# Order of the products in the first mixture of experts: latents and context in groups of four row blocks

## The chip, the cores and the metric

The kernel runs on one core of one Trainium2 chip. The metric is the device time of one launch in microseconds (us). Before the change three runs took 2783.61, 2788.53 and 2795.34 us; the median is 2788.53 us. The engines are named as in the profile: PE is TensorE (matmuls), PEld its weight loads, DVE is VectorE, ACT is ScalarE, POOL is GpSimd, SP is SyncE, which here only issues DMAs.

## The reference, cut to what matters

The model is a two-layer hybrid backbone on 512 latent tokens and 256 context tokens of width 1024, all in float32. Layer 0 mixes tokens with neighbourhood attention, layer 1 with a bidirectional recurrence; after each comes a mixture of experts with 16 experts. Each expert chooses the tokens it likes best: 64 latents (2 * 512 / 16), and in layer 0 also 32 context tokens (2 * 256 / 16) with the same weights. Layer 1 has no mixture for the context. What one expert computes:

```
xin = h[idx]                                   # 64 latents, or 32 context tokens, of width 1024
hid = silu(xin @ w1) * (xin @ w3)              # w1, w3: 1024 x 1024
y   = (hid @ w2) * gate                        # w2: 1024 x 1024; then added back at the rows idx
```

The weights of one expert are three 1024 x 1024 float32 matrices, 12 MiB; all 16 experts are read in full in each layer.

## The kernel before

The program runs in four stages: neighbourhood attention, the first mixture (layer 0, latents and context), the recurrence, the second mixture (layer 1, latents only). The change touches `expert` alone (lines 744 to 811), which both mixtures call. In the second one `xinc` is None, so there are no context products.

**Weights.** `load_weights` brings one tile `wm` of 1 MiB: two row blocks of 128 rows (two values of k) of one matrix. An expert has twelve of them: numbers 0 to 7 are w1 and w3 by turns, 8 to 11 are w2. Its caller issues the load of tile i + 10 from SP right behind the matmuls that read tile i, because in the first mixture the tiles lie in a ring of ten buffers. A load can start only when the last reader of the tile ten places before it is done. SP takes its loads in order.

**The first two products.** For every k of 0 to 7 the latents' part of `expert` makes four matmuls (line 759): w1 into P1 and w3 into P3, each in two halves of 512 columns. The stationary operand is 64 columns wide (64 latents), so the two halves stand side by side in two column tiles of the array and write PSUM partitions 0 to 63 and 64 to 127. The context's part (line 763) makes four matmuls into Pc with 32 stationary columns each, in four column tiles side by side. The stationary operands are slices of `xin` and `xinc`, gathered and transposed tokens. In the profile every float32 matmul shows as two records, so one k is 8 records of line 759 and 8 of line 763.

**Between them.** ACT takes the SiLU of P1 (line 768), DVE multiplies by P3 (line 769), PE transposes the result (line 71, `tp` from `hid`), ACT copies it to `hidT` (line 774). For the context the same with `hidc` (lines 777, 778) and `hidTc` (line 783).

**The third product.** For every k two matmuls for the latents (line 792, 4 records) and four of 256 columns for the context (line 796, 8 records).

**Around it.** Every second expert `gather` fetches the next 128 latents, every fourth the next 128 context tokens. `scatter` (line 829, 128 stationary columns) adds the results back into the rows.

**Who sets the order.** The code gives each engine a program order, but the instructions of this stage are laid out by a planner at build time: it goes through a modelled time line and gives an engine the earliest instruction, in program order, whose inputs the model holds ready. So matmuls of a later line are found ahead of an earlier one that was not ready in the model. The order is fixed before the run; the chip executes it as it stands. The recurrence has its order for PE, DVE and ACT written by hand.

Of the kernel before, what the change touches and what calls it, by code (L numbers as in the profile page):

```python
# [33 lines left out]
KD = 8  # L34
# [34 lines left out]
def transpose(S, out, in_):  # L69
    n = in_.shape[0]  # L70
    S.nc.tensor.transpose(out, in_, S.ident[:n, :n])  # L71
# [550 lines left out]
def load_weights(S, R, i, q=None):  # L622

    e, j = divmod(i, 12)
    if e >= E:
        return
    n, kk = (("moe_w1", "moe_w3")[j % 2], j // 2) if j < 8 else ("moe_w2", j - 8)
    a = R.ring[i % len(R.ring)]
    w = R.wm[a].tile([P, 2, D], F32, name="wm")
    (q or S.nc.sync).dma_start(w, S.I[n][R.l, e, kk * 256:(kk + 1) * 256].rearrange("(k p) n -> p k n", p=P))  # L630
    R.w[i] = w
# [112 lines left out]
def expert(S, R, e, xin, xinc, wk, psh, Y, YC):  # L744
    nc = S.nc
    ctxs = xinc is not None
    P1 = psh.tile([P, 512], F32, name="P1")
    P3 = psh.tile([P, 512], F32, name="P3")
    Pc = psh.tile([P, 512], F32, name="Pc") if ctxs else None
    cl = slice(64 * (e % 2), 64 * (e % 2) + 64)  # L750
    cc = slice(32 * (e % 4), 32 * (e % 4) + 32)
    for kk in range(4):
        ws = [R.w.pop(12 * e + 2 * kk + i) for i in range(2)]
        for k2 in range(2):
            k = 2 * kk + k2
            st, sp = k == 0, k == KD - 1
            for w, ps in zip(ws, (P1, P3)):
                for hf in range(2):
                    nc.tensor.matmul(ps[64 * hf:64 * hf + 64], xin[:, k, cl], w[:, k2, hf * 512:(hf + 1) * 512],  # L759
                                     start=st, stop=sp)  # L760
            if ctxs:
                for i in range(4):
                    nc.tensor.matmul(Pc[32 * i:32 * i + 32], xinc[:, k, cc],  # L763
                                     ws[i // 2][:, k2, (i % 2) * 512:(i % 2 + 1) * 512], start=st, stop=sp)
        for i in range(2):
            load_weights(S, R, 12 * e + 2 * kk + i + len(R.ring))
    hid = wk.tile([P, 512], F32, name="hid")
    nc.scalar.activation(hid, P1, AF.Silu)  # L768
    nc.vector.tensor_tensor(hid, P3, hid, op=ALU.mult)  # L769
    pt = S.ps_tp.tile([P, 512], F32, name="tp")  # L770
    for c in range(4):
        transpose(S, pt[:, c * P:(c + 1) * P], hid[:, c * P:(c + 1) * P])
    hT = wk.tile([P, 4, 2, CAPL], F32, name="hidT")
    nc.scalar.activation(hT.rearrange("p c h s -> p (c h s)"), pt, AF.Copy)  # L774
    if ctxs:
        hc = wk.tile([P, 512], F32, name="hidc")
        nc.scalar.activation(hc[64:128], Pc[0:64], AF.Silu)
        nc.vector.tensor_tensor(hc[0:64], Pc[64:128], hc[64:128], op=ALU.mult)
        pt = S.ps_tp.tile([P, 512], F32, name="tp")
        for c in range(4):  # L780
            transpose(S, pt[:, c * 64:(c + 1) * 64], hc[0:64, c * P:(c + 1) * P])
        hTc = wk.tile([P, 4, 2, CAPC], F32, name="hidTc")
        nc.scalar.activation(hTc.rearrange("p c h s -> p (c h s)"), pt[:, :256], AF.Copy)
    py = S.ps_mm.tile([P, 512], F32, name="mm")
    pyc = S.ps_mm.tile([P, 512], F32, name="mm") if ctxs else None
    for kk in range(4):
        w = R.w.pop(12 * e + 8 + kk)
        for k2 in range(2):
            k = 2 * kk + k2
            st, sp = k == 0, k == KD - 1  # L790
            for hf in range(2):
                nc.tensor.matmul(py[64 * hf:64 * hf + 64], hT[:, k % 4, k // 4, :], w[:, k2, hf * 512:(hf + 1) * 512],  # L792
                                 start=st, stop=sp)
            if ctxs:
                for i in range(4):
                    nc.tensor.matmul(pyc[32 * i:32 * i + 32, :256], hTc[:, k % 4, k // 4, :],
                                     w[:, k2, i * 256:(i + 1) * 256], start=st, stop=sp)
        load_weights(S, R, 12 * e + 8 + kk + len(R.ring))
    o = 64 * (e % 2)
    for hf in range(2):  # L800
        r = slice(64 * hf, 64 * hf + 64)
        c = slice(512 * hf, 512 * hf + 512)
        nc.vector.scalar_tensor_tensor(Y[o:o + 64, c], py[r], R.g[0][r, e:e + 1], S.gt2[0][r, c],  # L803
                                       op0=ALU.mult, op1=ALU.mult)
    if ctxs:
        o = 32 * (e % 4)
        for i in range(4):
            r = slice(32 * i, 32 * i + 32)
            c = slice(256 * i, 256 * i + 256)
            nc.vector.scalar_tensor_tensor(YC[o:o + 32, c], pyc[r, :256], R.g[1][r, e:e + 1], S.gt2[1][r, c],  # L810
                                           op0=ALU.mult, op1=ALU.mult)
# [21 lines left out]
def phase_moe(S, R):  # L833
    tc, l = S.tc, R.l
    ctxs = l == 0
    with ExitStack() as es:
        n0, n1 = WRING[l]
        R.wm.append(es.enter_context(tc.tile_pool(name="wmq", bufs=n1, reuse_waits="tile")))
        wk = es.enter_context(tc.tile_pool(name="moew", bufs=2, reuse_waits="tile"))
        R.ring += [len(R.wm) - 1] * n1  # L840
        m = max(n0, EARLY[l])
        for i in range(n0, m):
            load_weights(S, R, i)
        with tc.issue_after(R.last.ins):
            for i in range(m, n0 + n1):
                load_weights(S, R, i, S.nc.gpsimd)
        psh = es.enter_context(tc.tile_pool(name="psh", bufs=1, space=PSUM))
        xc = None
        for e in range(E):
            if e % 2 == 0:  # L850
                xl = gather(S, R, e // 2, 0)
                Y = wk.tile([P, D], F32, name="Y")
            if e % 4 == 0 and ctxs:
                xc = gather(S, R, e // 4, 1)
                YC = wk.tile([P, D], F32, name="YC", bufs=1)
            expert(S, R, e, xl, xc, wk, psh, Y, YC if ctxs else None)
            if e % 2 == 1:
                scatter(S, R, wk, R.ids[0][:, e // 2:e // 2 + 1], Y, S.X[:NLT])
            if e % 4 == 3 and ctxs:
                scatter(S, R, wk, R.ids[1][:, e // 4:e // 4 + 1], YC, S.X[NLT:])  # L860
    R.es.close()
# [1050 lines left out]
```

## Time and profile before

| what | value |
|---|---|
| median of three runs | 2788.53 us (2783.61 to 2795.34) |
| the profiled execution's own time | 2783.66 us |
| its span in the profile | 2781.7 us |
| PE busy, share of the span | 2475.8 us, 89% |
| DVE, ACT, POOL busy | 48%, 36%, 21% |
| granted TensorE clock, mean | 0.955 of full speed |
| bytes moved by DMA | 637.62 MB, 229 GB/s over the span |
| first mixture, first to last product | 631.5 us to 1284.5 us |
| second mixture, end of the last products of line 759 | 2757.2 us |

The span is the first to the last instruction of one profiled execution; its own time is 2 us longer and includes what lies around the span. A busy time is the time in which an engine had at least one instruction under way. For PE that says little about speed, since matmuls overlap and their ends are modelled, so below the distance from the start of one group of matmuls to the start of the next is read.

### The profile page before, as it was taken

The numbers are of one execution on the slowest core, as the hardware profiler recorded it, in microseconds if no ns is written. First come the engines' busy times: TensorE is split into PE (matmuls) and PEld (weight loads), VectorE is DVE, ScalarE is ACT, GpSimd is POOL, SyncE is SP. The second block draws the span as 40 slices with busy tenths as digits, with TensorE's granted clock in tenths as the row PEclk, the third lists the DMA queues.
The fourth block names the chain that finished last, engine by engine and source line by source line (L and its number), as shares of the span: only waits on it lengthen the run. The fifth ranks groups of instructions, "written<-read, shape, count | busy, mean of one in ns | idle before, by whom it ended". The sixth has DMA issues, their size and how long they took to land. (4 is left out here: it accounts for less than half of the span.)

```text
span 2781.7 us, 43985 instructions
## 1 busy us (share of the span) xinstructions
PE 2475.8 (89%) x16803; PEld 1534.7 (55%) x16803; DVE 1337.5 (48%) x2987; ACT 1004.4 (36%) x2121; POOL 595.9 (21%) x855
## 2 busy tenths in 40 slices
PE   6999999889999999997689697999999959988887
PEld 4876778782333322333389596777778843322222
DVE  6656665551222211215978745676676762211221
ACT  3555566531110100113266535676665421000000
POOL 1110000121000000001556535665555200000000
PEclk9999999989999999998899898999999959999999
DMA  8655530329788879774157966556654279999998
GB/s 244 146 157 183 159 114 17 113 103 372 271 345 319 325 287 364 277 292 166 69 176 247 270 158 136 130 127 145 129 115 127 61 274 373 409 409 409 409 409 334
DMA packets 427521, 637.62 MB, mean 229 GB/s; under 512 B 133824, under 2 KB 301056, under 8 KB 427312
## 3 DMA queue, kind: packets, MB, share of 16 engines
q1 hardware_dynamic: 419328, 609.11, 64.7%
q0 software_dynamic: 7984, 25.70, 2.5%
q8 instruction: 134, 2.20, 0.3%
q14 instruction: 75, 0.61, 0.1%
HBM read 565.11 MB, written 53.88 MB: 223 GB/s over the span
## 5 line engine op out<-in xcount | busy, mean ns | idle before, releaser
L759 PE MATMUL P<-wm,xin 128*64 128x512 f32 x2048 | 503.3, 607 | 42.1 <-DMA wm<-in_moe_w_dram 41.9
L759 PEld LDWEIGHTS P<-wm,xin 128*64 128x64 f32 x2048 | 132.8, 137 | 369.8 <-issue 270.8
L792 PE MATMUL mm<-wm,hidT 128*64 128x512 f32 x1024 | 250.8, 601 | 20.4 <-ACT hidT L774 16.1
L768 ACT ACTIVATE hid<-P 128x512 f32<-128x512 f32 x32 | 19.1, 598 | 690.1 <-PE P L759 690.1
L803 DVE SCALAR_TENSOR_TENSOR Y<-mm,gates,gt 64x512 f32<-64x512 f32 x64 | 48.0, 750 | 320.8 <-PE mm L792 320.1
L769 DVE TENSOR_TENSOR hid<-P,hid 128x512 f32<-128x512 f32 x32 | 22.1, 692 | 371.3 <-PE P L759 371.3
L731 POOL DMA_INDIRECT xg<-xnd,ii x20 | 19.1, 956 | 808.1 <-PE tp L71 521.9
L248 PE MATMUL mm<-wh,hTh 128*128 128x256 f32 x576 | 171.6, 298 | 2.5 <-ACT hTh L542 2.5
L250 PE MATMUL mm<-wh,hTl 128*128 128x256 f32 x576 | 166.7, 290 | 1.7 <-DVE hTl L545 1.7
L249 PE MATMUL mm<-wl,hTh 128*128 128x256 f32 x576 | 166.7, 290 | 0.0
L792 PEld LDWEIGHTS mm<-wm,hidT 128*64 128x64 f32 x1024 | 69.0, 136 | 159.5 <-issue 116.4
L763 PE MATMUL Pc<-wm,xin 128*32 128x512 f32 x1024 | 147.3, 602 | 0.0
L1443 POOL TENSOR_TENSOR Wi<-Wi,Ti 112x30 f32<-112x30 f32 (+14 forms) x240 | 142.1, 592 | 18.7
L1441 POOL TENSOR_TENSOR Ti<-Wi 112x30 f32<-112x30 f32 (+14 forms) x240 | 135.8, 566 | 18.2
L248 PEld LDWEIGHTS mm<-wh,hTh 128*128 128x128 f32 x576 | 112.5, 195 | 12.7 <-issue 9.1
L250 PEld LDWEIGHTS mm<-wh,hTl 128*128 128x128 f32 x576 | 112.0, 195 | 4.2 <-DVE hTl L545 2.7
L1520 PE MATMUL mm<-FR,QF 128*128 128x128 f32 (+1 forms) x768 | 113.5, 291 | 0.4 <-ACT QF L1508 0.4
L249 PEld LDWEIGHTS mm<-wl,hTh 128*128 128x128 f32 x576 | 112.6, 196 | 1.4 <-issue 1.4
L830 DVE TENSOR_TENSOR X<-mm,X 128x512 f32<-128x512 f32 x80 | 51.9, 687 | 106.1 <-PE mm L829 105.8
L1520 PEld LDWEIGHTS mm<-FR,QF 128*128 128x128 f32 x768 | 97.1, 197 | 7.4 <-ACT QF L1508 0.9
L1508 ACT ACTIVATE QF<-mm 64x256 f32<-64x256 f32 x192 | 72.9, 379 | 66.8 <-PE mm L1504 63.1
L1523 DVE TENSOR_TENSOR FT<-mm,eye 64x128 f32<-64x128 f32 x192 | 55.9, 292 | 77.4 <-ACT FT L1522 75.4
(429 smaller groups left out, 5697.3 us busy)
## 6 DMA issues: line engine op xcount, KB each, us to landing
wm<-in_moe_w_dram SPq DMA_DIRECT2D x378, 1024.0 KB
adaw<-in_ada_w_dram SPq DMA_DIRECT2D x96, 512.0 KB
wraw<-in_na_w_qkv_dram SPq DMA_DIRECT2D x32, 256.0 KB
wm<-in_moe_w_dram POOLq DMA_DIRECT2D x6, 1024.0 KB, 11.0
pkd<-sig SPq DMA_DIRECT2D x24, 256.0 KB
pkd<-kka SPq DMA_DIRECT2D x24, 256.0 KB
pkd<-av SPq DMA_DIRECT2D x24, 256.0 KB
sig<-pkd SPq DMA_DIRECT2D x16, 384.0 KB
```

Source lines behind the costliest of these rows:

```text
L248: S.nc.tensor.matmul(ps, xh, wh, start=(k == 0), stop=False)
L249: S.nc.tensor.matmul(ps, xh, wl, start=False, stop=False)
L250: S.nc.tensor.matmul(ps, xl, wh, start=False, stop=(k == n - 1))
L759: nc.tensor.matmul(ps[64 * hf:64 * hf + 64], xin[:, k, cl], w[:, k2, hf * 512:(hf + 1) * 512], start=st, stop=sp)
L763: nc.tensor.matmul(Pc[32 * i:32 * i + 32], xinc[:, k, cc], ws[i // 2][:, k2, (i % 2) * 512:(i % 2 + 1) * 512], start=st, stop=sp)
L792: nc.tensor.matmul(py[64 * hf:64 * hf + 64], hT[:, k % 4, k // 4, :], w[:, k2, hf * 512:(hf + 1) * 512], start=st, stop=sp)
L830: nc.vector.tensor_tensor(X[t][:, sl], ps, X[t][:, sl], op=ALU.add)
L1441: nc.gpsimd.tensor_tensor(t, W3[:, i + 1:32, i:i + 1].to_broadcast([112, n, i]), W3[:, i:i + 1, 0:i].to_broadcast([112, n, i]), op=ALU.mult)
L1443: nc.gpsimd.tensor_tensor(W3[:, i + 1:32, 0:i], W3[:, i + 1:32, 0:i], t, op=ALU.add)
L1508: nc.scalar.activation(QF[m][0:64, u], pq[64 * u:64 * u + 64], AF.Copy)
L1520: nc.tensor.matmul(pf[:, h, s0:], QF[m][:, u, h, :], rhs, start=True, stop=True)
L1523: nc.vector.tensor_tensor(F[64:128, :, 64:128], pf[64:128, :, 64:128], S.eye2[64:128, None, :].to_broadcast([64, 2, 64]), op=ALU.add)
```

## The change

`expert` gets a step: 4 where the context is computed, 2 where it is not. In a step the latents' matmuls of all its k come first, then the context's matmuls of the same k, then the loads that reuse the buffers of the step. Before, the turn changed at every k, and loads were issued after every second k, two tiles in the first two products (lines 765 and 766) and one for w2 (line 798). With a step of 4 four tiles are given back at once in the first two products, and two in the third. The number of matmuls, their shapes and operands stay. Without the context the loops come out in the order that they had.

```diff
-    for kk in range(4):
-        ws = [R.w.pop(12 * e + 2 * kk + i) for i in range(2)]
-        for k2 in range(2):
-            k = 2 * kk + k2
-            st, sp = k == 0, k == KD - 1
-            for w, ps in zip(ws, (P1, P3)):
+    step = 4 if ctxs else 2
+    for k0 in range(0, KD, step):
+        ws = {k: [R.w[12 * e + 2 * (k // 2) + i][:, k % 2] for i in range(2)] for k in range(k0, k0 + step)}
+        for k in range(k0, k0 + step):
+            for w, ps in zip(ws[k], (P1, P3)):
                 for hf in range(2):
-                    nc.tensor.matmul(ps[64 * hf:64 * hf + 64], xin[:, k, cl], w[:, k2, hf * 512:(hf + 1) * 512],
-                                     start=st, stop=sp)
-            if ctxs:
+                    nc.tensor.matmul(ps[64 * hf:64 * hf + 64], xin[:, k, cl], w[:, hf * 512:(hf + 1) * 512],
+                                     start=k == 0, stop=k == KD - 1)
+        if ctxs:
+            for k in range(k0, k0 + step):
                 for i in range(4):
                     nc.tensor.matmul(Pc[32 * i:32 * i + 32], xinc[:, k, cc],
-                                     ws[i // 2][:, k2, (i % 2) * 512:(i % 2 + 1) * 512], start=st, stop=sp)
-        for i in range(2):
-            load_weights(S, R, 12 * e + 2 * kk + i + len(R.ring))
+                                     ws[k][i // 2][:, (i % 2) * 512:(i % 2 + 1) * 512], start=k == 0, stop=k == KD - 1)
+        for i in range(12 * e + k0, 12 * e + k0 + step):
+            del R.w[i]
+            load_weights(S, R, i + len(R.ring))
...
-    for kk in range(4):
-        w = R.w.pop(12 * e + 8 + kk)
-        for k2 in range(2):
-            k = 2 * kk + k2
-            st, sp = k == 0, k == KD - 1
+    for k0 in range(0, KD, step):
+        ws = {k: R.w[12 * e + 8 + k // 2][:, k % 2] for k in range(k0, k0 + step)}
+        for k in range(k0, k0 + step):
             for hf in range(2):
-                nc.tensor.matmul(py[64 * hf:64 * hf + 64], hT[:, k % 4, k // 4, :], w[:, k2, hf * 512:(hf + 1) * 512],
-                                 start=st, stop=sp)
-            if ctxs:
+                nc.tensor.matmul(py[64 * hf:64 * hf + 64], hT[:, k % 4, k // 4, :], ws[k][:, hf * 512:(hf + 1) * 512],
+                                 start=k == 0, stop=k == KD - 1)
+        if ctxs:
+            for k in range(k0, k0 + step):
                 for i in range(4):
                     nc.tensor.matmul(pyc[32 * i:32 * i + 32, :256], hTc[:, k % 4, k // 4, :],
-                                     w[:, k2, i * 256:(i + 1) * 256], start=st, stop=sp)
-        load_weights(S, R, 12 * e + 8 + kk + len(R.ring))
+                                     ws[k][:, i * 256:(i + 1) * 256], start=k == 0, stop=k == KD - 1)
+        for i in range(12 * e + 8 + k0 // 2, 12 * e + 8 + (k0 + step) // 2):
+            del R.w[i]
+            load_weights(S, R, i + len(R.ring))
```

## Rows read from the trace of the kernel before

**Rows 1.** Busy time of the engines in three stretches: the whole first mixture, its beginning, and the rest without the end. The columns are the stretch (us from the span's start), its length, busy us of PE, PEld, DVE, ACT and POOL with the count of instructions, then the granted clock, the busy share of the DMA engines and what they moved in GB/s.

```profile
631.00:1284.50 653.50, 645.51 (x3940) 198.87 (x3938) 136.47 (x224) 82.75 (x180) 14.16 (x17) 1.00 0.82 311
640.00:700.00 60.00, 58.46 (x349) 16.25 (x350) 6.18 (x10) 8.16 (x16) 0.98 (x1) 1.00 1.01 402
700.00:1240.00 540.00, 534.36 (x3252) 166.71 (x3248) 122.59 (x202) 69.02 (x152) 7.50 (x8) 1.00 0.83 314
```

**Rows 2.** Waits of PE from 640 to 1284 us, all that the view has: engine, line, what it waited for, then us in total, times, the longest.

```profile
PE mm L792 <- ACT hidT L774: 8.0, 10, 0.8
```

**Rows 3.** Waits of SP's queue and of the loads that follow, 600 to 1300 us, the same columns.

```profile
SPq L630 <- PE Pc L763: 363.2, 60, 43.1
SPq L630 <- PE mm L796: 188.8, 54, 15.7
SPq L996 <- DVE X L830: 37.8, 4, 32.6
```

**Rows 4.** Groups of instructions by line, 625 to 1300 us: the four products, with their shapes, counts, busy us, mean ns of one record, and idle time before them.

```profile
L759 PE MATMUL P<-wm,xin 128*64 128x512 f32 x1024 | 260.4, 608 | 0.0
L763 PE MATMUL Pc<-wm,xin 128*32 128x512 f32 x1024 | 147.3, 602 | 0.0
L792 PE MATMUL mm<-wm,hidT 128*64 128x512 f32 x512 | 133.0, 603 | 8.0 <-ACT hidT L774 8.0
L796 PE MATMUL mm<-wm,hidTc 128*32 128x256 f32 x1024 | 66.9, 383 | 0.0
```

**Rows 5.** PE in order of time, merged, in the sixth expert (number 5): start us, length us with the modelled end, engine, line, tiles, shape, count of records.

```profile
846.16 1.94 PE L759 MATMUL P<-wm,xin 128*64 128x512 f32 x8
848.03 1.06 PE L763 MATMUL Pc<-wm,xin 128*32 128x512 f32 x8
849.03 1.94 PE L759 MATMUL P<-wm,xin 128*64 128x512 f32 x8
...
860.48 1.94 PE L759 MATMUL P<-wm,xin 128*64 128x512 f32 x8
862.35 1.07 PE L763 MATMUL Pc<-wm,xin 128*32 128x512 f32 x8
863.35 0.66 PE L71 MATMUL tp<-ident,hid 128*128 128x128 f32 x4
864.77 1.51 PE L792 MATMUL mm<-wm,hidT 128*64 128x512 f32 x6 [0.77 <-ACT hidT L774]
```

**Rows 6.** PE in order of time at two places where three k stand together, in the order of the argument: expert 6 (P), then expert 4 (Pc) with a scatter behind it.

```profile
881.48 5.37 PE L759 MATMUL P<-wm,xin 128*64 128x512 f32 x24
886.78 1.05 PE L763 MATMUL Pc<-wm,xin 128*32 128x512 f32 x4
...
801.12 2.78 PE L763 MATMUL Pc<-wm,xin 128*32 128x512 f32 x24
803.83 1.07 PE L759 MATMUL P<-wm,xin 128*64 128x512 f32 x2
804.83 0.50 PE L829 MATMUL mm<-yh,pm 128*128 128x512 f32 x1
```

**Rows 7.** The first and the last group of the stage in PE's order of time; between them 474 groups are counted where neighbours of one line are taken as one: 136 of line 759, 125 of line 763, 56 of line 792, 49 of line 796, 59 transposes (line 71) and 49 scatters (line 829).

```profile
631.48 8.79 PE L759 MATMUL P<-wm,xin 128*64 128x512 f32 x30
...
1280.91 3.66 PE L796 MATMUL mm<-wm,hidTc 128*32 128x256 f32 x64
```

**Rows 8.** The third product in order of time: expert 4, whose context is ready and takes turns, then the start of expert 6's.

```profile
832.69 1.93 PE L792 MATMUL mm<-wm,hidT 128*64 128x512 f32 x6
834.55 0.64 PE L796 MATMUL mm<-wm,hidTc 128*32 128x256 f32 x8
835.12 1.07 PE L792 MATMUL mm<-wm,hidT 128*64 128x512 f32 x2
836.12 0.64 PE L796 MATMUL mm<-wm,hidTc 128*32 128x256 f32 x8
...
845.60 0.64 PE L796 MATMUL mm<-wm,hidTc 128*32 128x256 f32 x8
...
912.79 3.65 PE L792 MATMUL mm<-wm,hidT 128*64 128x512 f32 x14
916.37 1.50 PE L796 MATMUL mm<-wm,hidTc 128*32 128x256 f32 x24
917.80 1.07 PE L792 MATMUL mm<-wm,hidT 128*64 128x512 f32 x2
```

**Rows 9.** The third product of expert 7, whose context comes late.

```profile
944.36 6.22 PE L792 MATMUL mm<-wm,hidT 128*64 128x512 f32 x26 [0.83 <-ACT hidT L774]
950.51 0.46 PE L71 MATMUL tp<-ident,hidc 64*128 64x64 f32 x4
950.90 1.93 PE L792 MATMUL mm<-wm,hidT 128*64 128x512 f32 x6
953.34 3.66 PE L796 MATMUL mm<-wm,hidTc 128*32 128x256 f32 x64
```

**Rows 10.** The first two products in expert 1, in order of time.

```profile
682.94 1.08 PE L759 MATMUL P<-wm,xin 128*64 128x512 f32 x4
683.95 1.05 PE L763 MATMUL Pc<-wm,xin 128*32 128x512 f32 x4
684.93 1.94 PE L759 MATMUL P<-wm,xin 128*64 128x512 f32 x8
```

## The prediction, made before the changed kernel was run

> **What bounds the kernel now.** I read the stretches first, then the waits, then PE's order of time. In the first mixture, 653.5 us long, PE is busy for 645.51 us at the full granted clock of 1.00; DVE and ACT are busy for 136 and 83 us, and the DMA engines for 0.82 of the time [rows 1]. Only once, at the beginning (640 to 700 us), do they run at 1.01 and 402 GB/s; from 700 us on they have a sixth of their time to spare. PE's one wait is 10 times 0.8 us for `hidT` [rows 2], and no wait for a weight tile is in that view. So here PE sets the time, and SP waits for PE: 363.2 us for line 763 and 188.8 us for line 796, the last readers of a tile [rows 3]. The way into the recurrence hangs on the same end: the store of X waits for the last scatter [rows 3]. What PE saves in this stage should come off the whole.
>
> A busy PE is not a PE at work, so I look at the starts. In expert 5 a latents' block of one k goes from 846.16 to 848.03, 1.87 us, the context's from 848.03 to 849.03, 1.00 us, and so on to 862.35 [rows 5]. Where three k stand together, the latents' 24 records take 5.30 us (881.48 to 886.78) instead of 3 * 1.87 = 5.61, the context's 2.71 us (801.12 to 803.83) instead of 3.00 [rows 6]. Two changes of kind fewer save 0.31 and 0.29 us: **a change of kind costs 0.15 us**, and the products themselves take 1.72 us (latents) and 0.85 us (context) for a k.
>
> As a test: with 128 k, that is 128 * 1.72 + 136 * 0.15 = 240.6 us for line 759, and 128 * 0.85 + 125 * 0.15 = 127.6 us for line 763 (counts from [rows 7]). The busy times are 260.4 and 147.3 us [rows 4]; they count each group's modelled end besides (1.94 against 1.87 us), and groups in which one column tile stands empty. The price fits.
>
> **The change, part by part.**
>
> *First two products.* In program order an expert has 16 blocks now (P, Pc for each k) and 4 after. That would be 12 * 0.15 = 1.8 us an expert, 28.8 us in all. Not all of it is there to be had. The trace has 136 + 125 = 261 blocks of the two lines [rows 7]: some experts begin with three k together because `xinc` came late, others are cut by scatters and transposes. Such a piece between two long blocks of one kind cuts one of them, where now it often falls on a change that is there anyway. I count 4 * 16 = 64 blocks, some 45 cuts and some 12 more in expert 1 (below), 121. That takes away 140 changes of kind: **21 us** (bounds: 28.8, and 12 if the planner leaves twice as many cuts).
>
> The Trainium skill has a rule against it. The row first: in the blocks of 24 the stationary operand changes at every k, and nothing is lost at these places [rows 6]. "TensorE: Matmul & The Clock Gate", sections "Step-by-step: what each phase is for" and "The mechanism", lets a weight load run under a matmul in flight only if it goes to other rows of the array (or, in the first, to a background buffer). Taken strictly, with all 128 rows in use here, the pause would be the load of new stationary columns, which stays at every k, and the change would bring nothing. The trace speaks against that reading.
>
> *Third product.* Where the context's `hidTc` is ready, lines 792 and 796 take turns: from 832.69 to the end of the last block at 846.16 (the start of the next row of expert 5 [rows 5]) expert 4 changes sixteen times [rows 8]. Expert 6 starts with 14 and 24 records together, 3.58 and 1.43 us, and then takes turns [rows 8]. Where it comes late, as in expert 7, line 792 runs through and line 796 behind it, two kinds in all [rows 9]. I find turns in six even experts (4 to 14) and none in ten. In groups of four the six have four blocks each. Of the 56 + 49 = 105 blocks [rows 7] some 60 stay: 45 * 0.15 = **7 us** (bounds: 3 to 9).
>
> *Between them.* The 0.8 us for `hidT` in ten experts: after the change four k of the context, 4 * 0.85 us, run while ACT and DVE make `hid`, so the transposes find it done. But in program order they stand behind these blocks, and the copy to `hidT` comes behind the transposes as before (863.35 to 864.77 [rows 5]). I take 0; if the planner puts the transposes among the context's products, up to 8 us are gained [rows 2].
>
> *Expert 1.* While the tiles were late in the planner's model, it cut one k into w1 and w3: a group of 4 of line 763 takes 0.98 us, as long as a group of 8, since two of the four column tiles stand empty [rows 10]. The new order lets it take both k of a tile before it turns. I take 0; bounds 0 to 6 us gained (0.85 at seven of its eight k).
>
> *The loads.* Four tiles come back at once, and no earlier than the context's last k of the group: for the first two of them that is two k later. A tile takes 1.0486 MB / 402 GB/s = 2.6 us [rows 1]; an expert's twelve take 31.3 us of some 39 us. The tiles read last in the first two products (6 and 7) are asked for when 8 and 9 of the expert before are free, at the latest at its very end. They land some 5.2 us later; PE comes to them only after four k of both kinds and two of the latents, 4 * 2.57 + 2 * 1.72 + two changes = 14 us. Tiles 10 and 11 are asked for after those first four k, and needed after four more and the hidden layer, over 11 us later. So PE need not wait: 0. If this slack were gone, one tile late in each expert would cost 16 * 2.6 = 42 us. SP has nothing else in its queue in this stage that waits behind these loads; the store of X comes behind the last of them and waits for the scatter anyway [rows 3].
>
> *Second mixture.* Same order as before: 0. Recurrence: shifted as a whole, 0.
>
> **Sum:** 21 + 7 = 28 us. From the profiled execution's own 2783.66 us (span 2781.7 and 2 us around it) that leaves 2755.7 us. The median of the three runs lies 4.9 us higher, 2788.53, and would become 2760.5. I say 2759.
>
> **The rivals.**
> *The planner keeps the turns (2776).* Its model may hold tiles or `xinc` late and fill with the other kind; it did so in expert 1 [rows 10], and scatters come in many small pieces [rows 7]. Then perhaps 80 changes of kind go, 12 us. Against it: from expert 5 on it follows program order wherever nothing is missing [rows 5].
> *The weights come late (2803).* For it: most of SP's waiting is for line 763 [rows 3], the release that is now put off, and the DMA engines have 0.17 to spare, not more [rows 1]. It decides once tile 6 or 7 lands more than some 9 us later than reckoned; then one tile of 2.6 us in each expert, 42 us, against 28 gained: slower by 14. Against it: no wait for a tile now [rows 2].
> *The stationary load is the price (2788).* The pause stays at each k. Nothing in the time changes, against [rows 6]. That is the skill's rule above, read strictly.
> *More than reckoned (2744).* The halves of expert 1 and the wait for `hidT` go as well, 6 + 8 us.
>
> **How the numbers follow.** Chances: forecast 0.66, planner 0.14, weights 0.08, no price 0.04, more 0.08. The forecast's own range is 2748 to 2772 (12 + 3 to 28.8 + 9 us gained, with a few us of scatter between runs). For 8 in 10 I take 2742 to 2782: it holds the forecast, the gains beyond it and most of the planner's case. A measurement of this kernel tells about 0.5%, 14 us, from no change: that is 2774.6 and 2802.5. Faster: forecast and more, and a fifth of the planner's case, 0.77; the rest of that case and no price, 0.15; slower 0.08.
>
> **What would show it.** Blocks of 32 records in lines 759 and 763, 6.9 + 0.15 and 3.4 + 0.15 us from start to start; some 120 groups of the two lines instead of 261; busy time of lines 759 and 763 down by some 15 us each (70 groups by 0.15 us and the modelled end of 0.07); the same 1024 records; the stage some 625 us long, and the same distance from its end to the end of the kernel. Wrong if PE waits for `wm` in this stage, if a change inside a long block costs 0.15 us as well, or if the planner's blocks stay as short as they are.

## The result and the profile after

The changed kernel takes 2762.67 us (median of four runs, 2761.22 to 2765.37) against 2789.45 us before (median of four runs): a ratio of 0.9909 (95% interval 0.9892 to 0.9925). Two more comparisons, of programs with the same instructions in the same order, gave 0.9922 (0.9892 to 0.9951) and 0.9908 (0.9883 to 0.9933). By these ratios that is 22 to 26 us less; the forecast was 2759 us, 28 us less.

Where it went: I measure the first mixture from the start of the first latents' product to the start of the first scatter behind its last product. Before it is 631.48 to 1284.50, 653.0 us; after 630.57 to 1255.99, **625.4 us, 27.6 less**. The same stretches as in [rows 1], of the changed kernel:

```profile
630.00:1256.00 626.00, 618.05 (x3940) 216.66 (x3939) 136.75 (x224) 82.71 (x180) 14.27 (x17) 1.00 0.83 325
640.00:700.00 60.00, 58.47 (x367) 18.06 (x366) 6.18 (x10) 8.03 (x17) 0.98 (x1) 1.00 1.02 409
700.00:1240.00 540.00, 534.38 (x3411) 189.30 (x3413) 126.99 (x209) 69.62 (x154) 7.51 (x8) 1.00 0.83 324
```

The clock is 1.00 throughout as before, PE is as busy as before, and in the same 540 us it gets through 3411 records instead of 3252. The busy share of PE, 99% in both, tells nothing of the gain. Now expert 5 in order of time, which answers to [rows 5]:

```profile
842.99 7.09 PE L758 MATMUL P<-wm,xin 128*64 128x512 f32 x32
850.01 3.64 PE L763 MATMUL Pc<-wm,xin 128*32 128x512 f32 x32
853.58 0.66 PE L71 MATMUL tp<-ident,hid 128*128 128x128 f32 x4
855.01 6.22 PE L791 MATMUL mm<-wm,hidT 128*64 128x512 f32 x26 [0.77 <-ACT hidT L775]
```

Four k of the latents take 7.02 us from start to start, where four single blocks of 1.87 take 7.48; the context's four take 3.57 instead of 4.00. The groups of the stage by line, for [rows 4]:

```profile
L758 PE MATMUL P<-wm,xin 128*64 128x512 f32 x1024 | 250.1, 601 | 0.0
L763 PE MATMUL Pc<-wm,xin 128*32 128x512 f32 x1024 | 135.0, 597 | 0.0
L791 PE MATMUL mm<-wm,hidT 128*64 128x512 f32 x512 | 128.4, 597 | 7.9 <-ACT hidT L775 7.9
...
L796 PE MATMUL mm<-wm,hidTc 128*32 128x256 f32 x1024 | 62.3, 380 | 0.0
```

The same records of all four products, with 10.3, 12.3, 4.6 and 4.6 us less busy time. The wait for `hidT` is what it was. SP still waits for the last readers of the tiles, in line 763 more often than before, but for less time in all (65 times and 317.6 us, in [rows 3] 60 and 363.2):

```profile
SPq L630 <- PE Pc L763: 317.6, 65, 42.8
SPq L630 <- PE mm L796: 211.7, 55, 15.6
```

PE waits for no tile in this stage. From 640 to 1256 us its waits are one line, as in [rows 2]:

```profile
PE mm L791 <- ACT hidT L775: 7.9, 10, 0.8
```

**What was not expected is in the third product.** Expert 6 took turns there before [rows 8]. After:

```profile
897.04 5.31 PE L791 MATMUL mm<-wm,hidT 128*64 128x512 f32 x22
902.28 0.46 PE L71 MATMUL tp<-ident,hidc 64*128 64x64 f32 x4
902.67 2.36 PE L791 MATMUL mm<-wm,hidT 128*64 128x512 f32 x9
...
904.88 4.02 PE L758 MATMUL P<-wm,xin 128*64 128x512 f32 x15
908.83 0.62 PE L763 MATMUL Pc<-wm,xin 128*32 128x512 f32 x1
908.84 0.63 PE L796 MATMUL mm<-wm,hidTc 128*32 128x256 f32 x6
```

Line 791 runs through all eight k, and line 796 comes behind the next expert's products: not the groups of four of the code, but the pattern of [rows 9]. With four k of the context at the end of the first two products, `hidTc` is late in every expert. Where the end of line 791 meets the next expert's line 758, or line 763 meets line 796, both products have the same number of stationary columns. And expert 1 still cuts its k [rows 10]:

```profile
679.38 1.94 PE L758 MATMUL P<-wm,xin 128*64 128x512 f32 x8
681.25 1.04 PE L763 MATMUL Pc<-wm,xin 128*32 128x512 f32 x2
682.22 1.94 PE L758 MATMUL P<-wm,xin 128*64 128x512 f32 x8
```

### The profile page after: what moved, and what is told of

It reads as the page before. It is cut to its first block, busy times and chain, and to the rows that moved or that the text cites. A ratio compares the mean times of both kernels' runs of the same rounds, so it can differ in the third digit from the quotient of the medians.

```text
span 2763.6 us, 43998 instructions
## 1 busy us (share of the span) xinstructions
PE 2458.2 (89%) x16803; PEld 1561.9 (57%) x16803; DVE 1338.9 (48%) x2987; ACT 1003.4 (36%) x2121; POOL 594.5 (22%) x855
## 5 line engine op out<-in xcount | busy, mean ns | idle before, releaser
L758 PE MATMUL P<-wm,xin 128*64 128x512 f32 x2048 | 492.6, 603 | 42.0 <-DMA wm<-in_moe_w_dram 41.7
L758 PEld LDWEIGHTS P<-wm,xin 128*64 128x64 f32 x2048 | 139.4, 137 | 348.3 <-issue 249.4
L763 PE MATMUL Pc<-wm,xin 128*32 128x512 f32 x1024 | 135.0, 597 | 0.0
```

The lines of the kernel that those rows point to most:

```text
L763: nc.tensor.matmul(Pc[32 * i:32 * i + 32], xinc[:, k, cc], ws[k][i // 2][:, (i % 2) * 512:(i % 2 + 1) * 512], start=k == 0, stop=k == KD - 1)
```

## The experiments

Two counts of the program as laid out go with each run: **changes of width**, the places in PE's order of this stage where the stationary operand's columns change between 32, 64 and 128 (423 before, 235 after; transposes and scatters are 128 wide), and **cut groups**, the groups of line 763 whose number of matmuls is not a multiple of four, so that one to three of the four column tiles stand empty at their end (30 and 31). The theory is that a change of width costs (653.0 - 625.4) / (423 - 235) = 0.147 us, which agrees with the 0.15 us that the prediction read off [rows 5] and [rows 6]. The rivals: every change of product costs this, whatever its width; and the late return of the tiles makes PE wait.

All profiles, in us. "Stage" is the distance defined above, "rest" the one from its end to the end of the span, "time" the median with the count of runs:

| kernel | changes of width | stage | rest | time |
|---|---|---|---|---|
| before | 423 | 653.0 | 1497.2 | 2789.45 (4) |
| before, again | 423 | 652.5 | 1499.9 | 2786.26 (1) |
| after | 235 | 625.4 | 1507.6 | 2762.67 (4) |
| after, again | 235 | 625.3 | 1501.0 | 2762.88 (6) |
| first products only | 235 | 626.6 | 1512.8 | 2763.89 (4) |
| third product only | 377 | 643.0 | 1503.8 | 2782.12 (1) |
| groups of two | 303 | 640.6 | 1503.6 | 2777.06 (1) |
| groups of eight | 243 | 644.8 | 1498.1 | 2774.98 (1) |
| ring of 8 | 260 | 639.2 | 1502.5 | 2774.08 (1) |
| ring of 6 | 394 | 678.6 | 1499.3 | 2813.16 (1) |
| turns, 32 columns | 172 | 620.5 | 1504.0 | 2760.59 (4) |
| groups of four, 32 columns | 172 | 615.3 | 1512.7 | 2762.43 (4) |
| late context, 32 columns | 176 | 607.8 | 1496.3 | 2747.20 (6) |

The stage of one program repeats within about 1 us; the rest does not, as the first five rows show.

**Both kernels again.** No edit.

> The kernel before, unchanged, for a second profile. The first pair of profiles shows 27.6 us saved inside the first mixture, but only 18 us over the span: about 10 us are given back in the recurrence behind it, in which no instruction was changed. If that is the scatter of the recurrence from one execution to the next, the distance from the end of the first mixture to the end of the span, 1497.2 us in the first profile of before, comes out some 5 to 10 us longer here (1502 to 1507 us). If the change causes it (another alignment of the small DMAs of the recurrence), it is 1497 us again.

> The changed kernel again, for the interval and a second profile. Theory (each change between matmuls of another column width costs 0.147 us, 188 of them fewer): 27 us less than before, ratio 0.990. The first mixture 625.4 us as in the first profile. What follows it: 1507.6 us in the first profile; with scatter from one execution to the next, between 1497 and 1508.

The stage came out at 652.5 and 625.3 us. The rest was 1499.9 us for before and 1501.0 us for after, against 1497.2 and 1507.6 us the first time; a third profile of the same changed program ("first products only" in the table) has 1512.8 us. So the rest of one and the same program scatters over 12 us. Before's second profile came out between the two cases expected, 2.7 us above the first.

The scatter goes with the TensorE clock granted over an execution. In the stage it is above 0.99 in every profile. Over the whole span it is 0.953, 0.950 and 0.947 in the three profiles of the changed program, whose rests are 1501.0, 1507.6 and 1512.8 us, and 0.955 and 0.952 in the two of before (1497.2 and 1499.9). The whole times follow it too. At 0.951, four runs of before took 2787.36 to 2792.50 us and three of the changed program 2761.13 to 2763.90, which is 23 to 31 us apart. The median clock of the runs that list one is 0.951 for both programs (29 and 14 runs). So the 10 us between the first two rests need no effect of the change: the runs show nothing that is given back, though they can't exclude a few us. The planner did lay out the recurrence anew: in the traces, 70 of SP's 1034 DMAs behind the stage stand at another place. Why the clock differs from one execution to the next is not shown.

**The price: width or product?** The order of before, with the latents' matmuls cut to the context's width. Four column tiles stand side by side instead of two, so the column time is the same. The third product likewise (shortened):

```diff
-                for hf in range(2):
-                    nc.tensor.matmul(ps[64 * hf:64 * hf + 64], xin[:, k, cl], w[:, hf * 512:(hf + 1) * 512],
+                for q in range(4):
+                    hf, s = divmod(q, 2)
+                    nc.tensor.matmul(ps[32 * q:32 * q + 32], xin[:, k, cl.start + 32 * s:cl.start + 32 * s + 32],
+                                     w[:, hf * 512:(hf + 1) * 512],
                                      start=k == 0, stop=k == KD - 1)
```

> The order of before (turns at every k), but the latents' products cut into matmuls of 32 stationary columns in four column tiles, in all three products, so that latents and context have the same width. As laid out, PE has 504 groups in the first mixture (461 before) but only 172 changes of column width (423 before). Theory (the price is the change of width): 251 * 0.147 = 37 us less in the first mixture, near 616 us, without any grouping. Rival (the price is paid at every change of product, because of its stationary columns or its PSUM bank): 43 groups more, 6 us slower, 659 us. Second rival (twice as many matmul instructions are too many to issue): slower still.

> The groups of four of the changed kernel, with all latents' products in 32 columns: 290 groups (287 after), 172 changes of width (235 after). Theory (width): 63 * 0.147 = 9 us less than the changed kernel, the first mixture near 616 us, the same as with turns at every k. Rival (every change of product): as the changed kernel, 625 us.

The stretch of the stage, first with turns, then with groups of four:

```profile
629.93:1250.43 620.50, 613.30 (x5473) 221.92 (x5473) 138.28 (x224) 83.21 (x179) 13.70 (x16) 1.00 0.85 328
```

```profile
632.00:1247.60 615.60, 607.91 (x5475) 219.33 (x5473) 138.28 (x224) 83.19 (x180) 13.96 (x17) 1.00 0.86 331
```

Turns at every k with one width: 620.5 us, 32 less than before (616 expected), with more changes of product than before. The rival that prices every change of product is out (it gave 659), and so is the one that fears the number of instructions (5473 records instead of 3940). The groups of four came to 615.3 us, as the theory had it (616). Turns cost 5.2 us more than groups, at 504 - 290 = 214 more groups as laid out: by this count 0.024 us for a change of product at equal width, a sixth of a change of width. What such a change looks like, with turns in 32 columns:

```profile
840.53 0.60 PE L766 MATMUL Pc<-wm,xin 128*32 128x512 f32 x2
840.57 0.98 PE L761 MATMUL P<-wm,xin 128*32 128x512 f32 x2
840.96 0.60 PE L766 MATMUL Pc<-wm,xin 128*32 128x512 f32 x2
841.00 1.42 PE L761 MATMUL P<-wm,xin 128*32 128x512 f32 x8
```

Each product here starts 0.04 to 0.4 us behind the start of the one before and runs beside it. With 64 against 32 columns none does. At all 190 changes between lines 759 and 763 in the trace of before, the next product starts 0.52 us behind the last start of the other, where inside a block the next round of matmuls, one record in each column tile, starts 0.41 to 0.42 us behind it. That is 0.10 to 0.11 us more, and the first round of a block takes 0.02 to 0.05 us longer than the later ones: together 0.14 to 0.15 us, the price read a second way. Ends of matmuls are modelled in the profile, so whether the array is empty in between can't be read from it.

The trace agrees with a rule that the Trainium skill states in "TensorEngine Tiling (Array Packing)", section "Key Properties": changing the tiling mode, not only the tile, drains the engine. It gives no price; here it is 0.147 us at the full clock. In the whole time the two kernels came out at 2760.59 and 2762.43 us, 0.991 (0.9878 to 0.9941) each, no better than the changed kernel: their 5 and 10 us in the stage are of the size of the scatter of the rest. All four runs with groups of four and 32 columns had a low clock, 0.947 or 0.948. They took 2759.64 to 2763.89 us, where the changed program's four runs at 0.946 or 0.947 took 2766.65 to 2775.90. So at a like clock the stage's gain shows; whether the low clock was chance is not shown.

**Which of the two edits?** First the one, then the other set back to turns at every k (shortened to the line that matters):

```diff
-    step = 4 if ctxs else 2          # third product
+    step = 1 if ctxs else 2          # third product; a tile is given back after two k
```

> Groups of four in the first two products alone; the third product takes turns at every k, in the code. As laid out, the instructions of every engine stand in the very order of the changed kernel: with the context's second four k at the end, hidTc is late in every expert, and line 791 runs through before line 796 whatever the code says. Theory: the first mixture 625.4 us, the time of the changed kernel (2762 us); the prediction's separate 7 us for the third product belong to the first two. Prediction's own split: 7 us more than the changed kernel, 632 us.

```diff
-    step = 4 if ctxs else 2          # first two products
+    step = 1 if ctxs else 2          # first two products; two tiles are given back after two k
```

> Groups of four in the third product alone, turns at every k in the first two. Laid out: 377 changes of column width in the first mixture, 423 before. Theory: 46 * 0.147 = 6.8 us less, the first mixture 646.0 us (652.8 before). Rival (the third product's turns hide behind something): 652.8 us.

The first gives the changed kernel's order (PE's and SP's instructions stand in the same order in both traces) and its stage (626.6 us). So in company the third product's edit does nothing. Alone it does what its code says, here in expert 4, where [rows 8] takes turns:

```profile
834.73 3.65 PE L796 MATMUL mm<-wm,hidT 128*64 128x512 f32 x16
838.31 1.93 PE L801 MATMUL mm<-wm,hidTc 128*32 128x256 f32 x32
840.18 3.65 PE L796 MATMUL mm<-wm,hidT 128*64 128x512 f32 x16
843.76 1.93 PE L801 MATMUL mm<-wm,hidTc 128*32 128x256 f32 x32
845.62 1.94 PE L760 MATMUL P<-wm,xin 128*64 128x512 f32 x8
```

10.89 us for eight k, where turns took 13.47 (832.69 to 846.16). In the stage it saves 9.7 us rather than 6.8, against the mean of before's two profiles. Eight fewer groups of the latents' third product end with an odd matmul, one column tile empty; half a block of 0.86 us for each, as below, is 3.4 us, and 6.8 + 3.4 = 10.2.

**How long may a group be?** `step` at 2 and at 8 in all products.

> Groups of two k instead of four, in all products; tiles are given back two at a time as before. Laid out: 303 changes of column width. Theory: 120 * 0.147 = 17.6 us less than before, the first mixture 635.2 us. Rival (what brings the time is that whole groups of four let the planner keep expert 1 and the waits apart): no simple rule, closer to 625 or to 652 us.

> Groups of all eight k, in all products: eight of the ten tiles are given back at once. Laid out: 243 changes of column width, 8 more than with groups of four, because the planner's model finds tiles late. Theory: 625.4 + 8 * 0.147 = 626.6 us for the first mixture, if no tile is late on the chip. Rival (weights come late): PE waits for wm show up, at one 2.6 us tile in each expert 42 us, some 668 us.

Both missed, to the same side: 640.6 instead of 635.2, and 644.8 instead of 626.6. Both have more cut groups of the context than before, 46 and 58 instead of 30. With groups of eight, expert 2:

```profile
727.37 1.94 PE L760 MATMUL P<-wm,xin 128*64 128x512 f32 x8
729.24 1.04 PE L765 MATMUL Pc<-wm,xin 128*32 128x512 f32 x2
730.21 1.94 PE L760 MATMUL P<-wm,xin 128*64 128x512 f32 x8
732.08 6.20 PE L765 MATMUL Pc<-wm,xin 128*32 128x512 f32 x50
```

A group of two records, one matmul in one of the four column tiles, takes 0.97 us from start to start, nearly what a whole k of eight takes (1.00, [rows 5]). Two parts instead of a whole cost 0.85 us more, so a cut group costs 0.43 on average. For groups of two that adds 16 * 0.43 = 6.9 us: 642.1, measured 640.6. For groups of eight, with 27 more than the changed kernel, 27 * 0.43 = 11.6 us: 638.2. There PE waits for tiles as well:

```profile
PE mm L796 <- ACT hidT L777: 9.8, 13, 0.8
PE P L760 <- DMA wm<-in_moe_w_dram: 3.1, 3, 1.1
```

That is 3.1 us for `wm` and 1.8 more for `hidT` than in [rows 2], 643.1; 2 us are left.

The empty column tiles can also be counted in the traces themselves. A matmul of 512 columns holds its column tile for 0.86 us (its two records start 0.43 us apart), one of 256 for half of that. Each block of one width is rounded up to full use of all its column tiles. By this estimate the tiles that stand empty cost 30.0 us before and 30.0 in the changed kernel, so the 27.6 us do not come from fuller column tiles. With groups of two they cost 34.3 and with groups of eight 43.7 us. The sums become 653.0 - 17.6 + 4.3 = 639.7 and 626.6 + 13.7 + 4.9 = 645.2 us, both within 1 us of the measured stage.

So the late return of the tiles does cost time, but mostly at the planner's desk: the order that it lays out cuts the context's k in two, and the chip executes that order with little waiting for tiles of its own. That the planner's model holds the tiles late is inferred from these orders; the ring, below, bears it out.

**How near are the tiles to being late?** The changed kernel with a smaller ring:

```diff
-WRING = {0: (0, 10), 1: (9, 6)}
+WRING = {0: (0, 8), 1: (9, 6)}
```

> The changed kernel with a ring of 8 weight tiles instead of 10, so that four of eight are given back at once. Laid out: 260 changes of width, and 60 groups of the context's matmuls that leave two of the four column tiles empty at their end (before 30, changed kernel 31; such a group costs 0.43 us more than its matmuls). Theory (the chip's tiles come in time, only the planner's order pays): 25 changes and 29 such groups more than the changed kernel, and 14 fewer that leave a column tile empty in line 791: 3.7 + 12.5 - 6.0 = 10 us more, the first mixture 635 us, no wait of PE for wm. Rival (tiles late on the chip): waits for wm of several 2.6 us, 650 us and more.

> The changed kernel with a ring of 6 weight tiles. Laid out: 394 changes of width, 109 groups of the context with empty column tiles. Here the weights must come late: with four of six tiles held, two can be under way, 5.2 us of transfer. Order alone: 159 * 0.147 + 78 * 0.43 - 28 * 0.43 = 45 us more than the changed kernel, 670 us; tiles late on the chip: on top of it waits of PE for wm, at one 2.6 us tile in each expert 42 us, 712 us.

With 8 tiles the stage takes 639.2 us, no wait for `wm` is among PE's waits, and the wait for `hidT` has grown from 8.0 to 12.5 us, which accounts for the 4 us above the 635 expected. The order laid out has 60 cut groups instead of 31. With 6 tiles it takes 678.6 us:

```profile
PE mm L796 <- ACT hidT L777: 12.1, 16, 0.8
...
PE P L760 <- DMA wm<-in_moe_w_dram: 2.5, 1, 2.5
```

2.5 us for a tile in this view and 5.9 us in that of the weight loads, not 42; the order alone was to bring it to 670. With 4.2 us more for `hidT` than in the changed kernel and 2.5 for `wm` that is 677; 2 us are left. So with groups of four the chip's transfers have room down to eight tiles, and the room that counts is the model's.

**A version that beats both.** One width for all products; the context's k 0 and 1 behind the latents' first four, its k 2 to 7 behind the last four; and the latents' hidden layer written ahead of them, so that its transposes may stand among the context's matmuls (shortened):

```diff
+    for l0, l1, c0, c1 in (((0, 4, 0, 2), (4, 8, 2, 8)) if ctxs else [(k, k + 2, k, k + 2) for k in range(0, KD, 2)]):
+        for k in range(l0, l1):
+            ws[k] = [R.w[12 * e + 2 * (k // 2) + i][:, k % 2] for i in range(2)]
+            lat(k, ws[k])
+        if l1 == KD:
+            hid = wk.tile([P, 512], F32, name="hid")
...
+        if ctxs:
+            for k in range(c0, c1):
+                con(k, ws[k])
```

> The best that the readings suggest: all latents' products in 32 columns as in g4_32; the context's products of k 0 and 1 behind the latents' first four k, those of k 2 to 7 behind the latents' last four, and SiLU, product and transposes of the latents' hidden layer written ahead of them. Laid out, the transposes of hid stand among the context's matmuls in most experts. Theory: the ten waits for hidT of 0.8 us go, 8 us, and the rest stays as in g4_32 (615.3 us): 607 us, and 2755 us in all, if six tiles given back at once do not make PE wait for wm. Rival (the wait for hidT moves to hidTc or to wm): 615 us or more.

The stage took 607.8 us, 607 expected, and the whole 2747.20 us (2737.93 to 2755.80): 0.9854 of before (0.9827 to 0.9880), clear of the changed kernel's intervals, though only just (the lowest begins at 0.9883), and the two were not run in one comparison; before took 2791.77 us in this one. In expert 5:

```profile
837.40 4.46 PE L755 MATMUL Pc<-wm,xin 128*32 128x512 f32 x36
841.79 0.66 PE L71 MATMUL tp<-ident,hid 128*128 128x128 f32 x4
842.38 1.48 PE L755 MATMUL Pc<-wm,xin 128*32 128x512 f32 x10
843.27 0.60 PE L796 MATMUL mm<-wm,hidT 128*32 128x512 f32 x2
```

The transposes stand among the context's matmuls and the third product follows without a gap; of the ten waits for `hidT` one is left:

```profile
PE mm L796 <- ACT hidT L770: 0.7, 1, 0.7
```

The whole time gained 44.6 us, the stage 45.2 (653.0 to 607.8).

## Why the prediction was right, point by point

- *The bound.* Right: PE nearly without waits at the full clock, and what this stage lost came off the whole as far as the runs can tell, 27.6 us in the stage, 22 to 26 in the three ratios and 23 to 31 between runs at one clock.
- *A change of kind costs 0.15 us.* Right in size, and now with its cause: the change of column width (0.147 us), not the change of product (0.024 us at equal width). The prediction's test by busy times could not tell the two apart, and it fits less well than it says: from start to start lines 759 and 763 take 251.0 and 136.8 us, 10 and 9 more than its sums, which it left to empty column tiles without counting them.
- *First two products, 21 us; third, 7 us.* The sum of 28 was right (27.6), its split was not. Summed from start to start, lines 758 and 763 take 16.6 us less (251.0 and 136.8 before, 244.1 and 127.1 after), lines 791 and 796 take 11.0 less (128.1 and 62.6, then 119.5 and 60.2), above the bounds of 3 to 9. The busy times of the first two lines fell by 10.3 and 12.3 us, not by 15 each. That the sum came out is in part luck. The prediction counted changes of kind, 140 + 45 = 185 fewer. As laid out 174 groups went (461 to 287), and in the trace the first two lines have 146 groups where 121 were forecast, the third product's 61 where it said 60. What the price goes by are changes of width, and 188 of those went, because more neighbours of equal width now stand side by side: line 791 beside 758, line 763 beside 796. The third product runs through instead of in groups of four, and all of this hangs on the first edit.
- *The planner keeps the turns (the rival at 2776).* Out: blocks of 32 records stand in the trace, and the stage lost 27.6 us, not 12.
- *The stationary load as the price.* Out, by the blocks of 32 records: four stationary operands in 7.02 us, which is the columns' 4 * 1.72 and one change. Behind the first round, the rounds of these blocks start 0.43 us apart, at the changes of k as elsewhere. The strict reading of the Trainium skill ("TensorE: Matmul & The Clock Gate", "The mechanism") does not hold here; the background buffer that its section "Step-by-step: what each phase is for" allows for would fit, but no run here shows that buffer. The prediction names the buffer for that section alone; "The mechanism" in the Trainium skill mentions it as well, in its opening paragraph.
- *Between them, 0.* Right: 7.9 us of waits for `hidT` after, 8.0 before. The last run shows that they could be had, and what it takes.
- *Expert 1, 0.* Right for this kernel: 31 cut groups in the stage instead of 30. But that term is what decided the groups of two and eight.
- *The loads, 0.* Right on the chip. The rival had the mechanism in the wrong place: tiles given back late are felt first in the order that the planner lays out, as cut groups, and only with eight tiles held or a ring of six as waits of PE, 3.1 and 2.5 us.
- *Recurrence, shifted as a whole.* Not quite: its DMAs were laid out in another order, and its end came 10 us later against the stage in the first pair of profiles. That goes with the granted clock (0.955 and 0.950); no time could be shown for the new order.

## What to carry to other kernels

Where matmuls of different stationary widths take turns, price the change from the trace (start to start of a long block against short ones) and count the changes; either group them, or cut the wider ones to the narrower width, so that turns become nearly free and buffers return early. When a planner lays out the order, a change in when buffers return acts through its model first: look in the new order for products cut in two before looking for waits on the chip. A stage that repeats within 1 us in every profile tells more of an edit than the whole time, when the rest scatters by 12; compare whole times at a like granted clock.

## What the runs showed of the hardware that was not expected

Twice as many float32 matmuls with half the stationary columns, four column tiles side by side instead of two, cost nothing: 32 records of line 761 with 32 columns, two k, take 3.4 us from start to start (839.55 to 842.98 with groups of four in 32 columns), as two k of 64 columns do (2 * 1.72):

```profile
839.55 3.64 PE L761 MATMUL P<-wm,xin 128*32 128x512 f32 x32
842.98 0.59 PE L766 MATMUL Pc<-wm,xin 128*32 128x512 f32 x1
```

And products of equal width overlap across a change: two matmuls of line 761 start 0.04 us behind the start of two of line 766, and run beside them.
